# RMS scaling of x one pass earlier, block sums ahead of their splits, a buffer of its own for the seventh block, and earlier evictions in the mixing layer's projections

## The chip, the core and the metric

One core of a Trainium2 chip runs the whole layer as one program. TensorE (PE) multiplies, ScalarE (ACT) and VectorE (DVE) prepare operands and take results out of PSUM, the queue of SyncE (SP) starts the loads from HBM. The metric is the time of the program on the device in microseconds, as the median of several runs. The profiled execution is one more run, with a trace of its own.

## What is computed

A decoder layer of width 2048 over 256 tokens, in float32: a SwiGLU feed-forward of hidden width 5632 at half weight, a mixing layer with one input projection for two groups of heads (RWKV-7 and a gated linear recurrence) and one output projection, a second SwiGLU, and a last RMS norm.

```python
def rms_norm(x, g):
    return x * lax.rsqrt(jnp.mean(x * x, axis=-1, keepdims=True) + NORM_EPS) * g

def swiglu(x, w_gate, w_up, w_down):
    return (jax.nn.silu(x @ w_gate) * (x @ w_up)) @ w_down

h = x
h = h + 0.5 * swiglu(rms_norm(h, ffn1_norm), ffn1_w_gate, ffn1_w_up, ffn1_w_down)
p = rms_norm(h, mix_norm) @ w_in
y_rwkv = rwkv7_time_mix(p[..., :RWKV_IN], ...)
y_lru = rglru_mix(p[..., RWKV_IN:], ...)
h = h + jnp.concatenate([y_rwkv, y_lru], axis=-1) @ w_out
h = h + 0.5 * swiglu(rms_norm(h, ffn2_norm), ffn2_w_gate, ffn2_w_up, ffn2_w_down)
return rms_norm(h, final_norm)
```

## The kernel before

**Products.** Every large product is made of three: an operand is split into a hi part (a cast to fp32r, called whi, xahi, hThi) and a lo part (the operand less its hi part: wlo, xalo, hTlo), and hi x hi, hi x lo and lo x hi are added in a PSUM bank (`three`, L136 to L138; `rows_times`, L174 to L177; `columns_times`, L186 to L188). For a weight, ACT casts (L81, L99) and DVE subtracts (L82, L100). One matmul has 512 columns, or 256 in the mixing layer's projections.

**The feed-forward.** `ffn` runs over the hidden width in chunks: a first one of 512, then five of 1024. In the first chunk the gate product runs over all 16 k tiles (`rows_times`, two k tiles to a split of 1024 columns), then the up product. A further chunk has a gate pass and an up pass of eight pairs of k tiles each, in the order n S n S n S n n. An n step is the plain product of a pair: its halves X1 and X2 are split one after the other, 12 matmuls each. An S step is a product of 2x2 blocks with seven products in place of eight, 21 matmuls. It needs sums of blocks of x (xsums) and of weight blocks (t1 to t4, made by DVE at L125, L127, L128). Its splits are A (b11 and b21), b22 alone (512 columns), C (t1 and t3) and D (t2 and t4); TensorE uses them in this order. After the last S step, DVE and ACT move the shared products into sg or hid (L300 to L304), and at a pass's end the pass's own banks are added (L317, L324). The hidden chunk is transposed by TensorE (L263) and split into hThi and hTlo (L270, L271) in the next chunk's gate pass. Then comes the down product, all with `rows_times`.

**Scaling.** x times its gain is transposed and split before its sum of squares is known. The first chunk's gate pass uses it unscaled, and its Silu (L340) scales by rstd. When the sums of squares are there (L233, `rstd_of`), `spread_rstd` makes rdiag on DVE (L203), a matmul with ones spreads rstd over the partitions (L204) and DVE copies it as rb (L206). In the first chunk's up pass `normalised` takes the pairs of k tiles one by one: DVE adds hi and lo (L279) and multiplies by rb (L280), ACT casts the new hi (L281), DVE subtracts the new lo (L282). For the three pairs of S steps, DVE and ACT go on with the block sums (L286 to L292). The up pass itself still reads unscaled x; its eviction (L351) multiplies by rstd.

**Order and buffers.** A scheduler puts each engine's instructions in order by priority; weight loads, splits and sums have an offset of 4000 over the rest. The order is fixed before the run, and each engine works its list in order. The tiles wst (loads of two k tiles, and t1 to t4), whi and wlo each come from a ring of three buffers (`wpool`). A load waits until the tile three back in its ring has been read.

**The mixing layer.** A projection of four tiles of 128 columns each runs over all k tiles; then DVE multiplies its banks by rb: L571 (raw; for k, r, v of a half of the heads), and in `lru_gate` L935. Between the splits, DVE also does the recurrences: a reciprocal of 128x1024 (L921, twice), a scan (L928) and the inverses of the RWKV part (L754, L758).

## Time and profile before

| | us |
|---|---|
| median of 3 runs | 1953.26 |
| their range | 1949.84 to 1953.41 |
| the profiled execution | 1948.99 |
| its span, first to last instruction | 1947.3 |
| TensorE busy in the span | 1907.3 (98%) |
| VectorE busy | 1440.3 (74%) |
| ScalarE busy | 985.8 (51%) |

By stage, in us of the span: ffn1's first chunk to 62, its passes with S steps from 62 to 503, its down product to 755, the mixing layer's projections and recurrences to about 1140, its output projection and ffn2's first chunk to about 1260, ffn2's S steps to 1700, its down product and the last norm to the end.

How to read it: a matmul's duration in the trace is longer than the distance to the next one, since they are pipelined, so TensorE's busy share does not tell how much of its time is lost. The number of matmuls that start in a stretch does.

### The profile page before, as it was taken

The page shows a single profiled execution, that of the slowest core. Times are in us where ns is not written, and L with a number is a line of the kernel's source. Part 1 is how long each engine was busy: PE and PEld are TensorE (multiplying, and loading weights), DVE is VectorE, ACT ScalarE, POOL GpSimd, SP SyncE. Part 2 cuts the span into 40 slices and gives each one's busy share as a digit, 9 for nine tenths or more (in the row PEclk, how much of TensorE's full clock was granted, in tenths as well). Part 3 has the DMA queues.
Part 4 walks back from the last instruction along what each step waited for, and adds up shares of the span by engine and source line. Part 5 has one row for each costly group of instructions (what it writes and reads, how often), then busy time and mean ns, then how long its engine had stood idle before and what let it go on. Part 6 is the DMA issues. An engine that isn't in the chain of part 4 may idle for free.

```text
span 1947.3 us, 25669 instructions
## 1 busy us (share of the span) xinstructions
PE 1907.3 (98%) x10233; PEld 1589.7 (82%) x10233; DVE 1440.3 (74%) x1822; ACT 985.8 (51%) x1189; POOL 9.9 (1%) x53
## 2 busy tenths in 40 slices
PE   8899999999999999999999999999999999999997
PEld 6678877878888889998899878778888888788886
DVE  5989898888645446876696775899898989844553
ACT  6465555555444335544454555565556555543443
POOL 0000000000000001000000000000000000000000
PEclk9999999999999999999999999999999999999999
DMA  6356555565755556545243456555555655766553
GB/s 238 129 198 214 173 194 195 178 212 190 264 186 204 194 195 207 177 127 163 77 144 115 131 195 215 173 194 182 199 197 198 211 183 184 257 211 193 195 194 129
DMA packets 130032, 360.77 MB, mean 185 GB/s; under 512 B 20879, under 2 KB 23128, under 8 KB 129784
## 3 DMA queue, kind: packets, MB, share of 16 engines
q1 hardware_dynamic: 129592, 358.08, 55.6%
q8 instruction: 80, 1.31, 0.3%
q10 hardware_dynamic: 320, 1.06, 0.1%
q14 instruction: 40, 0.33, 0.0%
HBM read 351.25 MB, written 7.86 MB: 184 GB/s over the span
## 4 chain that ended last, share of the span: by engine, by line
PE 89%; DVE 5%; ACT 3%; issue 2%; DMA 1%; SPq 0%; ACTq 0%; DVEq 0%
PE bank L137 14%; PE bank L136 13%; PE bank L138 13%; PE bank L175 10%; PE bank L177 10%; PE bank L174 10%; PE bank L186 4%; PE bank L188 4%; PE bank L187 4%; ACT whi L99 1%; DVE wlo L82 1%; PE bank L263 1%; DVE wlo L100 1%; PE bank L712 1%; PE bank L640 1%
## 5 line engine op out<-in xcount | busy, mean ns | idle before, releaser
L82 DVE TENSOR_TENSOR wlo<-wst,whi 128x1024 fp32r<-128x1024 f32 (+2 forms) x329 | 398.2, 1212 | 344.6 <-ACT whi L81 343.9
L99 ACT CAST whi<-wst 128x1024 fp32r<-128x1024 f32 (+1 forms) x440 | 430.4, 993 | 364.0 <-PE bank L138 321.9
L81 ACT CAST whi<-wst 128x1024 fp32r<-128x1024 f32 (+2 forms) x329 | 343.2, 1044 | 472.5 <-PE bank L177 335.8
L100 DVE TENSOR_TENSOR wlo<-wst,whi 128x1024 fp32r<-128x1024 f32 (+1 forms) x440 | 493.3, 1147 | 90.9 <-ACT whi L99 85.0
L174 PE MATMUL bank<-whi,hThi 128*128 128x512 f32 x704 | 274.2, 389 | 0.0
L175 PE MATMUL bank<-wlo,hThi 128*128 128x512 f32 x704 | 274.0, 389 | 0.0
L177 PE MATMUL bank<-whi,hTlo 128*128 128x512 f32 x704 | 231.4, 389 | 0.0
L186 PE MATMUL bank<-xahi,whi 128*128 128x256 f32 x688 | 199.1, 290 | 3.2 <-DVE raw L571 3.2
L188 PE MATMUL bank<-xahi,wlo 128*128 128x256 f32 x688 | 197.9, 288 | 0.0
L136 PE MATMUL bank<-whi,xahi 128*128 128x512 f32 x490 | 191.4, 393 | 6.3 <-ACT xahi L281 4.6
L187 PE MATMUL bank<-xalo,whi 128*128 128x256 f32 x688 | 197.3, 287 | 0.0
L137 PE MATMUL bank<-wlo,xahi 128*128 128x512 f32 x490 | 191.5, 391 | 0.6 <-DVE wlo L100 0.6
L136 PE MATMUL bank<-whi,xbhi 128*128 128x512 f32 x490 | 190.2, 391 | 1.9 <-DVE hid L351 1.4
L137 PE MATMUL bank<-wlo,xbhi 128*128 128x512 f32 x490 | 191.1, 390 | 0.6 <-DVE wlo L100 0.6
L138 PE MATMUL bank<-whi,xalo 128*128 128x512 f32 x490 | 191.4, 391 | 0.0
L138 PE MATMUL bank<-whi,xblo 128*128 128x512 f32 x490 | 190.7, 389 | 0.0
L175 PEld LDWEIGHTS bank<-wlo,hThi 128*128 128x128 f32 x704 | 132.2, 188 | 27.4
L177 PEld LDWEIGHTS bank<-whi,hTlo 128*128 128x128 f32 x704 | 132.1, 188 | 27.4
L174 PEld LDWEIGHTS bank<-whi,hThi 128*128 128x128 f32 x704 | 132.2, 188 | 27.1
L186 PEld LDWEIGHTS bank<-xahi,whi 128*128 128x128 f32 x688 | 133.1, 193 | 7.3 <-DVE raw L571 3.6
L188 PEld LDWEIGHTS bank<-xahi,wlo 128*128 128x128 f32 x688 | 132.9, 193 | 1.9 <-issue 1.1
L187 PEld LDWEIGHTS bank<-xalo,whi 128*128 128x128 f32 x688 | 133.1, 194 | 1.2 <-issue 0.2
(298 smaller groups left out, 2557.3 us busy)
## 6 DMA issues: line engine op xcount, KB each, us to landing
wst<-in_ffn_w_up_dram SPq DMA_DIRECT2D x88, 1024.0 KB, 5.0
wst<-in_ffn_w_down_dram SPq DMA_DIRECT2D x88, 1024.0 KB, 4.9
wst<-in_ffn_w_gate_dram SPq DMA_DIRECT2D x87, 1024.0 KB, 5.0
wst<-in_w_in_dram SPq DMA_DIRECT2D x40, 1024.0 KB, 5.0
wst<-in_w_out_dram SPq DMA_DIRECT2D x16, 1024.0 KB, 5.7
h<-parked SPq DMA_DIRECT2D x4, 1024.0 KB, 9.2
wst<-in_w_in_dram SPq DMA_DIRECT2D x4, 640.0 KB, 4.4
h<-in_x_dram SPq DMA_DIRECT2D x4, 512.0 KB, 4.7
```

The lines of the kernel that those rows point to most:

```text
L82: nc.vector.tensor_tensor(lo[:, : m * width], src, hi[:, : m * width].bitcast(F32), ALU.subtract)
L99: self.nc.scalar.copy(hv, src)
L100: self.nc.vector.tensor_tensor(lv, src, hv.bitcast(F32), ALU.subtract)
L136: nc.tensor.matmul(out, a[0], b[0], start=first, stop=False)
L137: nc.tensor.matmul(out, a[0], b[1], start=False, stop=False)
L138: self.last_mm = nc.tensor.matmul(out, a[1], b[0], start=False, stop=last)
L174: nc.tensor.matmul(banks[t][n][:, :w], a, whi[:, c : c + w], start=first, stop=False)
L175: nc.tensor.matmul(banks[t][n][:, :w], a, wlo[:, c : c + w], start=False, stop=False)
L177: self.last_mm = nc.tensor.matmul(banks[t][n][:, :w], b, whi[:, c : c + w], start=False, stop=last)
L186: nc.tensor.matmul(out, a, xhi[:, k, :], start=first, stop=False, skip_group_check=True)
L187: nc.tensor.matmul(out, a, xlo[:, k, :], start=False, stop=False, skip_group_check=True)
L188: nc.tensor.matmul(out, b, xhi[:, k, :], start=False, stop=last, skip_group_check=True)
```

## The change

- *Scaling.* The sums of squares, rstd and `normalised` move into the first chunk's gate pass, from k tile 6 on in ffn1 and from tile 0 on in ffn2. The block sums stay in the up pass (`block_sums`), from scaled pairs that are kept for them in four half tiles of sg and hid (`room`). The up pass now reads scaled x, so the eviction into hid no longer multiplies by rstd. The two loads of further norm gains in ffn1 move with the sums of squares.
- *S steps.* The three sums for t1 to t4 stand in the code before all four splits. b22 has a whi and a wlo tile of its own (tags whb and wlb, one buffer each), so an S step takes three tiles of each ring in place of four.
- *Mixing layer.* The evictions of projections (raw, xb, gate) get a priority offset of 3900. Each reciprocal of 128x1024 becomes four of 128x256.
- *Storage.* xa and xb are held as two halves with tiles of their own; the scrap tile of the sums of squares is float32 and shares its storage with hid. A path for S steps in the down product is there, but its plan is None for all pieces.

```diff
     def split(self, src, n):
-        hi = self.wpool.tile([P, self.WMAX], F32R, name=self.name("whi"), tag="whi")
-        lo = self.wpool.tile([P, self.WMAX], F32R, name=self.name("wlo"), tag="wlo")
+        pool = self.wpool if n == 2 else self.bpool
+        hi = pool.tile([P, n * 512], F32R, name=self.name("whi"), tag="whi" if n == 2 else "whb")
+        lo = pool.tile([P, n * 512], F32R, name=self.name("wlo"), tag="wlo" if n == 2 else "wlb")
...
                 else:
-                    b11, b21 = self.split(b[:, :, 0, :], 2)
-                    (b22,) = self.split(b[:, 1, 1:2, :], 1)
                     tt = self.wpool.tile([P, 2 * self.WMAX], F32, name=self.name("wst"), tag="wst")
                     t = tt.rearrange("p (n f) -> p n f", f=512)
                     nc.vector.tensor_tensor(t[:, 0:2], b[:, :, 1, :], b[:, 0], ALU.subtract)
-                    t1, t3 = self.split(t[:, 0:2], 2)
                     nc.vector.tensor_tensor(t[:, 2], t[:, 1], b[:, 0, 0, :], ALU.add)
                     nc.vector.tensor_tensor(t[:, 3], b[:, 1, 0, :], t[:, 2], ALU.subtract)
+                    b11, b21 = self.split(b[:, :, 0, :], 2)
+                    (b22,) = self.split(b[:, 1, 1:2, :], 1)
+                    t1, t3 = self.split(t[:, 0:2], 2)
                     t2, t4 = self.split(t[:, 2:4], 2)
...
+        norm_at, scaled = 6 if head else 0, 0
         for i, (k, hi, lo) in enumerate(core.weights([(wg, c0, w)], ks, head=bool(head))):
             core.rows_times(gb, xhi, xlo, k, hi, lo, w, i == 0, i == NK - 1)
             if head and i in head:
                 with core.tc.high_priority(offset=3000), core.tc.issue_after(core.last_mm.ins):
                     head[i]()
-        after_first()
-        sg = fpool.tile([P, NT, 1024], F32, name=core.name("sg"), tag="sg")
+            if i == norm_at:
+                after_first()
+                scrap = fpool.tile([P, NT, 1024], F32, name=core.name("sg"), tag="sg")
+                hid = fpool.tile([P, NT, 1024], F32, name=core.name("hid"), tag="hid")
+                sums = rest()
+            if i % 2 and i >= norm_at:
+                while scaled <= i // 2:
+                    normalised(scaled)
+                    scaled += 1
+        sg = scrap
...
-            if i == 0:
-                sums, scrap = rest(), sg
-            if i % 2:
-                normalised(i // 2)
-        hid = fpool.tile([P, NT, 1024], F32, name=core.name("hid"), tag="hid")
+            if i % 2 and i // 2 in place:
+                block_sums(room(i // 2), *sums(place[i // 2]))
         for t in range(NT):
             for n, c, ww in cuts:
-                nc.vector.scalar_tensor_tensor(
-                    hid[:, t, c : c + ww], ub[t][n][:, :ww], rstd[:, t : t + 1], sg[:, t, c : c + ww],
-                    ALU.mult, ALU.mult,
-                )
+                nc.vector.tensor_tensor(hid[:, t, c : c + ww], ub[t][n][:, :ww], sg[:, t, c : c + ww], ALU.mult)
...
-            nc.vector.tensor_tensor(
-                raw[:, :n, 1:257], bk[:, : n * 256].rearrange("p (a s) -> p a s", a=n), self.core.rb[:, None, :].to_broadcast([P, n, 256]), ALU.mult
-            )
+            with self.tc.high_priority(offset=3900):
+                nc.vector.tensor_tensor(
+                    raw[:, :n, 1:257], bk[:, : n * 256].rearrange("p (a s) -> p a s", a=n),
+                    self.core.rb[:, None, :].to_broadcast([P, n, 256]), ALU.mult,
+                )
...
-        nc.vector.reciprocal(D, D)
+        for j in range(4):
+            nc.vector.reciprocal(D[:, j * 256 : (j + 1) * 256], D[:, j * 256 : (j + 1) * 256])
```

The scheduler then puts the instructions in another order. The lists below are parts of it; the first number is the instruction's place on its engine, L the line in the kernel that the list is of, and the numbers behind names tell tiles apart.

TensorE about the start of ffn1's up pass, before: bank_140 is the last bank of the gate pass, bank_369 the first of the up pass, L204 spreads rstd.

```order
104 L175 MATMUL bank_140<-wlo_312,xahi 128x512
105 L177 MATMUL bank_140<-whi_311,xalo 128x512
106 L174 MATMUL bank_369<-whi_373,xahi 128x512
107 L175 MATMUL bank_369<-wlo_374,xahi 128x512
108 L177 MATMUL bank_369<-whi_373,xalo 128x512
109 L174 MATMUL bank_370<-whi_373,xahi 128x512
110 L204 MATMUL bank_349<-rdiag_348,ones 128x128 x2
111 L175 MATMUL bank_370<-wlo_374,xahi 128x512
```

The same place after: whi_326 is the gate pass's last split, whi_364 the up pass's first; L217 spreads rstd, L1137 transposes a norm gain.

```order
76 L217 MATMUL bank_278<-rdiag_277,ones 128x128 x2
77 L187 MATMUL bank_140<-whi_326,xahi_101 128x512
78 L188 MATMUL bank_140<-wlo_327,xahi_101 128x512
79 L190 MATMUL bank_140<-whi_326,xalo_103 128x512
80 L187 MATMUL bank_141<-whi_326,xahi_101 128x512
81 L188 MATMUL bank_141<-wlo_327,xahi_101 128x512
82 L190 MATMUL bank_141<-whi_326,xalo_103 128x512
83 L1137 MATMUL bank_287<-ident,graw_285 128x16
84 L187 MATMUL bank_140<-whi_364,xahi_101 128x512
```

The spreading matmul moved from behind four matmuls of the up pass to six matmuls ahead of it.

DVE about the start of ffn2's up pass, before: wlo_10540 and wlo_10544 are the gate pass's last splits, wlo_10596 and wlo_10600 the up pass's first, L206 makes rb.

```order
1180 L203 TENSOR_SCALAR rdiag_10580<-ident,rstd_96 128x128 x2
1181 L82 TENSOR_TENSOR wlo_10510<-wst_10503,whi_10509 128x1024
1182 L82 TENSOR_TENSOR wlo_10540<-wst_10537,whi_10539 128x1024
1183 L82 TENSOR_TENSOR wlo_10544<-wst_10537,whi_10543 128x1024
1184 L82 TENSOR_TENSOR wlo_10596<-wst_10593,whi_10595 128x1024
1185 L82 TENSOR_TENSOR wlo_10600<-wst_10593,whi_10599 128x1024
1186 L206 COPY rb_10586<-bank_10581 128x256
1187 L280 TENSOR_TENSOR sg_10588<-sg_10588,rb_10586 128x512
```

The same place after: wlo_10567 is the gate pass's last split, wlo_10605 and wlo_10609 the up pass's first; L312 adds hi and lo of a pair of x, L219 makes rb, L313 multiplies by it.

```order
1189 L97 TENSOR_TENSOR wlo_10567<-wst_10560,whi_10566 128x1024
1190 L238 SCALAR_TENSOR_TENSOR xblo_9810<-bank_10435,gT,xbhi_9808 128x256
1191 L255 TENSOR_SCALAR rt_10476<-rt_10476 128x2
1192 L312 TENSOR_TENSOR hid_10490<-xbhi_9808,xblo_9810 128x512
1193 L97 TENSOR_TENSOR wlo_10605<-wst_10602,whi_10604 128x1024
1194 L257 RECIPROCAL rstd_95<-rt_10476 128x2
1195 L216 TENSOR_SCALAR rdiag_10481<-ident,rstd_95 128x128 x2
1196 L219 COPY rb_10487<-bank_10482 128x256
1197 L97 TENSOR_TENSOR wlo_10609<-wst_10602,whi_10608 128x1024
1198 L313 TENSOR_TENSOR hid_10490<-hid_10490,rb_10487 128x512
1199 L313 TENSOR_TENSOR sg_10489<-sg_10489,rb_10487 128x512 x2
```

rb stands behind one split of the up pass where it stood behind two, and adds of pairs of x (there is one more above) stand ahead of it.

DVE in the S steps of ffn1's first full up pass, before: wlo_1062 and wlo_1066 are X1 and X2, wlo_1096 A, wlo_1100 b22, wlo_1106 C and wlo_1112 D of one n step and one S step; wst_1103 holds t1 to t4.

```order
142 L100 TENSOR_TENSOR wlo_1062<-wst_1059,whi_1061 128x1024
143 L100 TENSOR_TENSOR wlo_1066<-wst_1059,whi_1065 128x1024
144 L125 TENSOR_TENSOR wst_1103<-wst_1093 128x1024
145 L100 TENSOR_TENSOR wlo_1096<-wst_1093,whi_1095 128x1024
146 L127 TENSOR_TENSOR wst_1103<-wst_1103,wst_1093 128x512
147 L100 TENSOR_TENSOR wlo_1100<-wst_1093,whi_1099 128x512
148 L128 TENSOR_TENSOR wst_1103<-wst_1093,wst_1103 128x512
149 L100 TENSOR_TENSOR wlo_1106<-wst_1103,whi_1105 128x1024
150 L100 TENSOR_TENSOR wlo_1112<-wst_1103,whi_1111 128x1024
```

The same two steps after: wlo_1065 and wlo_1069 are X1 and X2, wlo_1103 A, wlo_1107 b22, wlo_1111 C, wlo_1115 D.

```order
142 L116 TENSOR_TENSOR wlo_1065<-wst_1062,whi_1064 128x1024
143 L136 TENSOR_TENSOR wst_1098<-wst_1096 128x1024
144 L116 TENSOR_TENSOR wlo_1069<-wst_1062,whi_1068 128x1024
145 L137 TENSOR_TENSOR wst_1098<-wst_1098,wst_1096 128x512
146 L116 TENSOR_TENSOR wlo_1103<-wst_1096,whi_1102 128x1024
147 L138 TENSOR_TENSOR wst_1098<-wst_1096,wst_1098 128x512
148 L116 TENSOR_TENSOR wlo_1107<-wst_1096,whi_1106 128x512
149 L116 TENSOR_TENSOR wlo_1111<-wst_1098,whi_1110 128x1024
150 L116 TENSOR_TENSOR wlo_1115<-wst_1098,whi_1114 128x1024
```

The first sum (L136) went ahead of X2 and the third (L138) ahead of b22. On ACT b22's cast (whi_1106) now stands ahead of A's, here after X1 and X2:

```order
94 L115 CAST whi_1064<-wst_1062 128x1024
95 L115 CAST whi_1068<-wst_1062 128x1024
96 L115 CAST whi_1106<-wst_1096 128x512
97 L115 CAST whi_1102<-wst_1096 128x1024
98 L115 CAST whi_1110<-wst_1098 128x1024
99 L115 CAST whi_1114<-wst_1098 128x1024
```

Before, A's cast (whi_1095) stood ahead of b22's.

## Rows read from the trace of the kernel before

**Rows 1.** The page's busy line: us (share of span) xinstructions.

```profile
PE 1907.3 (98%) x10233; PEld 1589.7 (82%) x10233; DVE 1440.3 (74%) x1822; ACT 985.8 (51%) x1189; POOL 9.9 (1%) x53
```

**Rows 2.** TensorE's waits: line, releaser, total us, times, longest.

```profile
PE bank L136 <- ACT xahi L281: 4.6, 1, 4.6
...
PE bank L186 <- DVE raw L571: 3.2, 2, 3.0
...
PE bank L175 <- DVE wlo L82: 2.2, 3, 1.1
```

**Rows 3.** TensorE by stretch: length, busy (matmuls), granted clock, DMA share, GB/s.

```profile
60.00:80.00 20.00, 12.97 (x47) 0.83 0.32 105
880.00:900.00 20.00, 16.95 (x117) 0.91 0.69 197
1260.00:1280.00 20.00, 18.67 (x76) 1.00 0.45 154
100.00:500.00 400.00, 399.07 (x1763) 1.00 0.60 198
1300.00:1700.00 400.00, 399.48 (x1764) 1.00 0.59 198
1760.00:1920.00 160.00, 160.00 (x708) 1.00 0.58 192
```

**Rows 4.** The same, transposes of L263 alone.

```profile
100.00:500.00 400.00, 9.05 (x72) 1.00 0.60 198
1300.00:1700.00 400.00, 8.27 (x69) 1.00 0.59 198
```

**Rows 5.** One S step in order of time: start, duration, engine, line, [idle before].

```profile
487.25 0.39 PE L136 MATMUL bank<-whi,xahi 128*128 128x512 f32 x1
...
489.29 0.61 PE L136 MATMUL bank<-whi,xsums 128*128 128x512 f32 x2
489.86 0.50 PE L137 MATMUL bank<-wlo,xsums 128*128 128x512 f32 x1
490.19 0.40 PE L138 MATMUL bank<-whi,xsums 128*128 128x512 f32 x1
...
487.49 1.05 ACT L99 CAST whi<-wst 128x1024 fp32r<-128x1024 f32 x1 [2.14 <-PE bank L138]
...
488.57 3.72 DVE L100 TENSOR_TENSOR wlo<-wst,whi 128x1024 fp32r<-128x1024 f32 x3 [1.55 <-ACT whi L99]
```

**Rows 6.** DVE by line and shape, 100 to 500 us: busy us, mean ns.

```profile
L100 DVE TENSOR_TENSOR wlo<-wst,whi 128x1024 fp32r<-128x1024 f32 x176 | 209.9, 1220 | 43.9 <-ACT whi L99 41.8
...
L128 DVE TENSOR_TENSOR wst<-wst,wst 128x512 f32<-128x512 f32 x27 | 18.5, 686 | 0.3
```

**Rows 7.** Loads of weights in the passes with S steps.

```profile
DMA to landing us min/median/max: 4.8/5.0/5.8
```

**Rows 8.** ffn1's first chunk on TensorE, in order of time.

```profile
38.97 0.68 PE L204 MATMUL bank<-rdiag,ones 128*128 128x128 f32 x4 [0.62 <-DVE rdiag L203]
...
63.04 0.47 PE L136 MATMUL bank<-whi,xahi 128*128 128x512 f32 x1 [1.69 <-DVE hid L351]
...
69.38 0.80 PE L136 MATMUL bank<-whi,xahi 128*128 128x512 f32 x1 [4.56 <-ACT xahi L281]
```

**Rows 9.** DVE by stretch: length, busy (instructions), granted clock, DMA share, GB/s.

```profile
20.00:40.00 20.00, 11.41 (x14) 1.00 0.52 163
100.00:500.00 400.00, 353.67 (x395) 1.00 0.60 198
1220.00:1240.00 20.00, 12.48 (x21) 1.00 0.63 198
```

**Rows 10.** ffn2's first chunk in order of time, DVE and then TensorE.

```profile
1236.87 0.42 DVE L206 COPY rb<-bank 128x256 f32<-128x256 f32 x1 [0.86 <-PE bank L204]
...
1260.02 0.47 PE L136 MATMUL bank<-whi,xbhi 128*128 128x512 f32 x1 [1.38 <-DVE hid L351]
...
1262.33 0.50 PE L136 MATMUL bank<-whi,xbhi 128*128 128x512 f32 x1 [0.51 <-ACT xbhi L281]
```

More of the change, by code (lines that the diff above doesn't have):

```diff
@@ L19, with __init__, __getitem__ @@
 EPS = 1e-6
+class Halves:
+    def __init__(self, *tiles):
+        self.tiles = list(tiles)
+    def __getitem__(self, at):
+        rows, k, cols = at
+        if isinstance(k, slice):
+            i, k = k.start // 8, slice(k.start % 8, k.start % 8 + k.stop - k.start)
+        else:
+            i, k = k // 8, k % 8
+        return self.tiles[i][rows, k, cols]
 class Core:
@@ L101, in split, with pairs @@
         return [(hi[:, i * 512 : i * 512 + 512], lo[:, i * 512 : i * 512 + 512]) for i in range(n)]
-    def pairs(self, mat, c0, plan):
+    def pairs(self, mat, c0, plan, ids):
         nc = self.nc
-        ns = plan.count("S")
-        ids = {"S": iter(range(ns)), "n": iter(range(ns, self.NK // 2))}
-        for kind in plan:
-            p = next(ids[kind])
+        for kind, p in zip(plan, ids):
             with self.tc.high_priority(offset=4000):
@@ L157, in rows_times_pairs @@
                 self.three(aux[0], x(0, 0), w["b11"], f, l)
-                self.three(own[1], sm(3), w["b22"], first, last)
-                self.three(aux[1], sm(0), w["t1"], f, l)
-                self.three(aux[3], sm(2), w["t3"], f, l)
-                self.three(aux[2], sm(1), w["t2"], f, l)
+                self.three(own[1], sm(4), w["b22"], first, last)
+                self.three(aux[1], sm(1), w["t1"], f, l)
+                self.three(aux[3], sm(3), w["t3"], f, l)
+                self.three(aux[2], sm(2), w["t2"], f, l)
                 self.three(own[2], x(1, 1), w["t4"], first, last)
@@ L243, in rstd_of, with ffn @@
         nc.vector.reciprocal(rstd, tmp)
-def ffn(core, xhi, xlo, rstd, wg, wu, wd, after_first, after_down, fpool, down, rest, back, head=None):
+def ffn(core, xhi, xlo, rstd, wg, wu, wd, after_first, after_down, fpool, down, rest, back, spare, head=None):
     nc, NT, NK, D, S = core.nc, core.NT, core.NK, core.D, core.S
@@ L1045 @@
 HIDDEN_AT = 6
+DOWN_PLAN, DOWN_HIDDEN_AT = (None, None, None), 2
 @with_exitstack
@@ L1084, in xt_pool, with half, sums @@
         pool = stack.enter_context(tc.tile_pool(name=name, bufs=1, **kw))
-        return [pool.tile([P, NK, S], F32R, name=name + n) for n in ("hi", "lo")]
+        def half(n, i):
+            return pool.tile([P, NK // 2, S], F32R, name=core.name(name + n), tag=f"{n}{i}")
+        def sums():
+            tiles = [pool.tile([P, 4, 512], F32R, name=core.name(name + "sum"), tag=f"{n}1") for n in ("hi", "lo")]
+            return lambda p: tuple(t[:, p % 4, :] for t in tiles)
+        return [Halves(half(n, 0), half(n, 1)) for n in ("hi", "lo")], half, sums
     with ExitStack() as front:
-        xa = xt_pool(front, "xa")
+        xa, xa_half, xa_sums = xt_pool(front, "xa")
         with ExitStack() as st:
```

139 lines of the change are left out of this document (91 added, 48 removed).

## The prediction, made before the changed kernel ran

> **What bounds the kernel now.** I read the page's busy line first: TensorE is busy for 98% of the span, VectorE (DVE) for 74%, ScalarE (ACT) for 51% [rows 1]. So the end is set by TensorE, and since the change leaves its matmuls as they are (8947 rows before, 8948 after, in the lists of instructions), all it can bring is TensorE time that is now lost. The list of what TensorE waited for says where the long waits are [rows 2]: one of 4.6 us for x scaled (L281), 3.2 us for a projection's eviction (L571), 2.2 us for weight splits, and others at the first hidden chunks. The list leaves out short waits, so I then counted matmuls by stretch [rows 3]. In a part of the down projection with nothing but matmuls of 512 columns, 708 start in 160 us, 0.226 us each. In the 400 us of passes with S steps in ffn1, 1763 start, of which 72 are transposes that take 9.05 us [rows 4]: 1691 x 0.226 + 9.05 = 391.2, so 8.8 us are lost. The same sum for ffn2 (1764, 69 transposes) gives 1695 x 0.226 + 8.27 = 391.3, 8.7 us lost. The two stretches with S steps are some 425 us long each, so about **19 us** go there, in pieces too short for the list.
>
> One S step shows the piece [rows 5]. The two L136 that open t1 and t3 start at 489.29 and 0.226 later, the next matmul (wlo of t1) should come at 489.74. It starts at 489.86, and the one after that 0.33 later instead of 0.23: 0.22 us lost. What it waited for is the subtraction that starts on DVE at 488.57 (1.22 us), behind the cast on ACT at 487.49, which had stood idle for 2.14 us for "PE bank L138": the whi buffer of C (t1, t3) is the one that the n step's second half (X2) holds until TensorE starts the S step. An S step takes four buffers (A: b11, b21; b22; C; D: t2, t4) of a ring of three. There are 60 S steps (3 in each of 20 passes): at 0.22 to 0.31 (the first of a pass loses a little more) 13 to 19 us, most or all of it.
>
> **The change part by part.**
>
> *Ring of three for three (S steps).* b22 gets its own buffer, so C takes the buffer of X1, free 12 matmuls (2.7 us) sooner, and D that of X2. Per pair n + S, TensorE needs 45 x 0.226 = 10.2 us. From the moment the matmul behind a buffer's last one starts (487.25 for X2) it is 0.24 to the cast's start, then 1.05 cast and 1.22 subtraction [rows 5], 2.5 us in all. D: X2 free at 0 (S step's start), ready at 2.5, wanted at 16 matmuls = 3.6. The next X1, in A's buffer: free at 1.4 (6 matmuls), ready 3.9, wanted 5.0. The next X2, in C's: free at 3.4, ready 5.9, wanted 7.7. So no buffer is late by itself: the margin is 1.1 us or more. What is late next is DVE: five splits and, as long as a split, the sum of 1024 columns, 6 x 1.22, and 3 x 0.69 for the others make 9.4 us of 10.2 per pair [rows 6], and in it the loop of the load. The pair's wst buffer is free when b22's subtraction ends; the load takes 5.0 us at the median, 5.8 at most [rows 7], so some 5.15 with its two signals; then, by the new order, come sum (1.14 start to start), X2's subtraction (1.14), sum (0.61), A (1.14), sum (0.61), b22 (0.61): 10.4 us against 10.2, where the old order (sum, A, sum, b22, sum behind X2) makes 9.3. A pass has three S steps and then two n steps that need no sums, and 3 x 0.2 stays under the margin of 1.1; but loads scatter, so I charge half the overshoot, 0.1, to each of 60 steps, 6 us, and 3 us for what stays at the passes' ends, where evictions and transposes wait for each other. Of 19 us **10 come back**; bounds 4 (the loop costs its 0.2 in full on each step, and the ends the same) and 15 (margins hold, only the ends stay).
>
> *x scaled in ffn1's first gate pass.* The count of matmuls in 60 to 80 us is 47, where 88 fit: 9.3 us lost [rows 3]. The waits there are 1.69 at 63.04 and 4.56 at 69.38 [rows 8]; of the rest, some 0.6 is a third wait and some 2.5 us TensorE at 1.2 GHz (granted clock 0.83 in that stretch) and restarts. Another microsecond goes at 38.97 [rows 8]. DVE had idled for 8.6 of the 20 us before 40 [rows 9], and only then got rb. By the order, the matmul that spreads rstd moves from the 4th matmul of the up pass to 6 before it, 10 x 0.226 = 2.3 us, and its own wait of 0.62 goes, since the split ahead of it on DVE ends 2.9 us before the up pass (its buffer is left 24 matmuls, 5.4 us, before the pass, and 2.5 us go from there to the subtraction's end). Two of the adds (0.69 each) are done before rstd is there. DVE is thus some 2.9 + 1.4 = 4.3 us ahead, and the waits of 6.8 us shrink by that; of the lost clock I give back 0.7. **5 us**, bounds 2 (the wait for pair 1's lo part, now behind more splits, takes over) and 8. The first gate pass still reads x unscaled, and its Silu still scales, so no instruction is added.
>
> First the row, for the clock: after the idle of 4.56 us and after that of 3.0 in front of L571 the granted clock of the stretch is 0.83 and 0.91; after 1.38 at 1260.02 it stays at 1.00 [rows 2, 3, 8, 10]. The Trainium skill (TensorE: Matmul & The Clock Gate, "HAM oscillation — how this bites in real kernels") says that idle gaps between bursts send the array back to half rate; by it a long wait that is left in ffn1 would keep the whole 2.5 us of clock loss, and this term would be 4.3.
>
> *The same in ffn2.* DVE idles 7.5 us of the 20 before 1240 [rows 9], and rb came at 1236.87 [rows 10]. By the order it stands behind the first split of the up pass instead of the second, and the spreading matmul 11 matmuls (2.5 us) ahead of the pass; there it waits some 0.3 us for that split. DVE is some 2.1 + 1.4 us ahead of before, and the waits at 1260.02 and 1262.33 [rows 10] with a smaller one between, 2.5 us, go, less the new 0.3: **2 us**, bounds 0 and 4.
>
> *Mix.* The evictions get a priority just under that of the splits. In the order the eviction behind the 3.2 us wait (k, second half) stands where it stood, between the same two splits: nothing there. The gate's evictions move ahead of the scan, and a reciprocal of 8x256 behind a split that waited 1.1 us [rows 2]; 0.4 of it goes and that wait also loses its restart. Each of the two long reciprocals becomes four with splits between; no long TensorE wait stands behind one now. Price of six more instructions: 2 x 0.69 - 1.22 = 0.16 each [rows 6], 1.0 us of DVE at most, nothing where DVE idles. Net **+0.5**, bounds -3 (one more wait like L571's, elsewhere) and +3.
>
> The Trainium skill (Perfetto Trace Analysis, "Optimizing Scalar/DVE Operations") puts an access overhead of some 60 ns on a DVE instruction and advises larger ones where the engine is saturated. By that estimate the six cost 0.4 us; the rows' 0.16 is more, and the measurement decides.
>
> *The rest.* Silu's partner at L351 loses a scalar operand; junk becomes f32 in another pool; the down path is the old one (its plan is None). No price: same instructions, same queues, ACT 51% busy.
>
> **Sum.** 10 + 5 + 2 + 0.5 = 17.5 us. Against the profiled execution (1948.99) 1931.5; the median of the runs lies 4.3 us above it, which would make 1935.8. I take **1933**.
>
> **The rivals.**
>
> *DVE and the load loop bind the S passes.* For: 9.4 of 10.2, a loop of 10.4. Against: DVE idles 46 us of 400 there [rows 9], and two n steps per pass let it catch up. Then S steps give 0 to 4 and the rest 7: 1940 to 1946, say 1943.
>
> *The scaling only moves its wait.* The sums stay in the up pass, and xalo of pair 1 is still behind weight splits. Then 10 + 0.5: 1942.
>
> *Slower: the sum ahead of the splits on an in-order DVE.* The first sum of an S step now stands ahead of X2's (in each pass's first S step of X1's) subtraction. If the load comes late, DVE waits for it with those subtractions queued behind, which TensorE wants first. With a load of 5.0 us it costs the 0.1 above. With 5.8, the longest of before, for all, the loop is 11.2, 1.0 over: 3 x 1.0 - 1.1 = 1.9 us on each of 20 passes, and the 3 at the ends, 41 us lost against 19 now, less 7.5 won elsewhere: 1953 + 22 - 7.5 = 1968. It decides where 3 times the overshoot less 1.1 is over 1.2, from a load of 5.6 us. Against it: the median is 5.0.
>
> *Everything fits*: 15 + 8 + 4 + 3 = 30: 1920.
>
> **How the numbers follow.** Forecast (1924 to 1940) 0.54; DVE binds 0.20; scaling moves its wait 0.12; all fits 0.07; slower 0.07. The range 1920 to 1948 takes in the upper end of the second case (4 + 2 + 0 - 3 = 3 us under the profiled run, rounded up toward the median); outside it are the slow case, and what no row shows. 0.2% is 3.9 us, about what a measurement can tell. Faster 0.85: all but the slow case and a piece of the second (0.08, no difference); slower 0.07.
>
> **What would show it.** In 100 to 500 us the matmuls should rise from 1763 to about 1784, without the pattern of 0.33 behind L137 of t1; if DVE's sum waits for a load there, the slow rival is at work. In 60 to 80 the count should rise from 47 to about 68; a wait of some 2 us for xalo would be the one that is left. At 1260 no wait over 0.5. The wait at L571 (3 us) should be there as before; were it gone, the order didn't tell what I read from it. Wrong would be the whole if the S stretches' count stays.

## The result and the profile after

The changed kernel takes **1931.38 us** (median of 4 runs, 1929.94 to 1935.32) where the kernel before takes 1952.19 (median of 4 beside it, 1949.84 to 1953.41): a ratio of 0.9898, 95% interval 0.988 to 0.9916. The profiled execution is the run of 1929.94, the shortest of the four, with a span of 1928.2.

The page's busy line, which answers to [rows 1]: TensorE is busy 12.2 us less, DVE and ACT within 2 us of before.

```profile
PE 1895.1 (98%) x10233; PEld 1598.7 (83%) x10233; DVE 1440.9 (75%) x1828; ACT 984.0 (51%) x1189; POOL 9.7 (1%) x53
```

TensorE's waits (line, releaser, total us, times, longest), which answer to [rows 2]:

```profile
PE bank L199 <- DVE raw L633: 3.6, 2, 3.1
...
PE bank L190 <- DVE xalo L315: 2.2, 1, 2.2
...
PE bank L217 <- DVE xalo L238: 1.5, 1, 1.5
...
PE bank L946 <- DVE rs L930: 1.0, 1, 1.0
```

The wait of 4.6 us for xahi is gone, and one of 2.2 for xalo is there in its place; the wait for the projection's eviction (L571 before, now L633) is what it was; L946 is new. L217, which spreads rstd, also waited before (L204):

```profile
PE bank L204 <- DVE xalo L225: 0.9, 1, 0.9
```

TensorE by stretch (length, busy and matmuls, granted clock, DMA share, GB/s), which answers to [rows 3]:

```profile
40.00:60.00 20.00, 17.85 (x72) 0.91 0.43 149
60.00:80.00 20.00, 20.00 (x89) 1.00 0.48 157
866.00:886.00 20.00, 16.95 (x110) 0.83 0.70 197
1260.00:1280.00 20.00, 20.00 (x89) 1.00 0.77 250
100.00:500.00 400.00, 399.53 (x1791) 1.00 0.59 204
1280.00:1680.00 400.00, 398.39 (x1782) 1.00 0.59 202
```

The same for the transposes of L280 alone (L263 before), which answers to [rows 4]:

```profile
100.00:500.00 400.00, 9.42 (x72) 1.00 0.59 204
1280.00:1680.00 400.00, 8.98 (x72) 1.00 0.59 202
```

The prediction's count of lost time, on these: in ffn1's S passes (1791 - 72) x 0.226 + 9.42 = 397.9, so 2.1 us of 400 are lost where 8.8 were; in ffn2's (1782 - 72) x 0.226 + 8.98 = 395.4, 4.6 lost where 8.7 were. The busy column (399.07 before, 399.53 after) shows nothing of that; the count of matmuls does.

Two S steps of the changed kernel, which answer to [rows 5] (start, duration, engine, line), at products with xsums:

```profile
157.83 0.50 PE L149 MATMUL bank<-whi,xsums 128*128 128x512 f32 x1
158.17 0.40 PE L150 MATMUL bank<-wlo,xsums 128*128 128x512 f32 x1
...
166.39 0.39 PE L149 MATMUL bank<-whi,xsums 128*128 128x512 f32 x1
166.62 0.39 PE L150 MATMUL bank<-wlo,xsums 128*128 128x512 f32 x1
166.84 0.39 PE L151 MATMUL bank<-whi,xsums 128*128 128x512 f32 x1
167.07 0.39 PE L149 MATMUL bank<-whi,xsums 128*128 128x512 f32 x1
```

From 166.39 on the starts are 0.23 apart through all four products, where before one was 0.33. At 157.83, in the last of the four, a piece of 0.11 is left (0.34 instead of 0.23).

By stages, from the starts of the same matmuls in each trace (us; "head" is up to the 66th matmul of the first chunk with S steps, in ffn2 counted from the start of the mixing layer's output projection; e2 to e11 are the experiments below):

| | before | after | e2 | e3 | e5 | e9 | e11 |
|---|---|---|---|---|---|---|---|
| ffn1 head | 85.8 | 79.0 | 80.2 | 79.0 | 75.3 | 89.3 | 77.4 |
| ffn1 S passes | 417.2 | 410.4 | 416.6 | 411.7 | 421.0 | 410.7 | 418.4 |
| ffn1 down | 243.1 | 243.0 | 243.0 | 243.0 | 243.0 | 243.0 | 243.0 |
| mixing, to its output projection's start | 368.3 | 371.3 | 370.2 | 370.1 | 369.5 | 375.2 | 374.6 |
| output projection and ffn2 head | 163.5 | 159.0 | 159.9 | 160.5 | 158.9 | 164.4 | 159.7 |
| ffn2 S passes | 416.7 | 412.4 | 416.4 | 412.7 | 418.5 | 413.0 | 420.1 |

What lies behind them is equal within 0.2 us. After against before: -6.8, -6.8, 0, +3.0, -4.4, -4.2, in all 19.2 us, the difference of the spans (1947.3 - 1928.2 = 19.1). Of the 4.4 us, 0.7 are the output projection's (98.1 us before, 97.5 after) and 3.7 those of ffn2's first chunk (65.2 and 61.5). e5's heads are short because its long wait comes behind the 66th matmul, in the S passes; there the two rows go together.

### The profile page after: what moved, and what is told of

It is laid out like the page before. It is cut to its first block, busy times and chain, and to the rows that moved or that the text cites. A ratio compares the mean times of both kernels' runs of the same rounds, so it can differ in the third digit from the quotient of the medians.

```text
span 1928.2 us, 25657 instructions
## 1 busy us (share of the span) xinstructions
PE 1895.1 (98%) x10233; PEld 1598.7 (83%) x10233; DVE 1440.9 (75%) x1828; ACT 984.0 (51%) x1189; POOL 9.7 (1%) x53
## 4 chain that ended last, share of the span: by engine, by line
PE 86%; DVE 8%; DMA 3%; issue 2%; ACT 1%; SPq 0%; DVEq 0%; ACTq 0%
PE bank L149 12%; PE bank L151 12%; PE bank L150 12%; PE bank L190 11%; PE bank L188 11%; PE bank L187 11%; PE bank L199 4%; PE bank L200 4%; PE bank L201 4%; DVE wlo L116 2%; DMA wst<-in_ffn_w_gate_dram 2%; DVE wlo L97 1%; PE bank L280 1%; PE bank L775 1%; DVE hid L365 1%
## 5 line engine op out<-in xcount | busy, mean ns | idle before, releaser
L116 DVE TENSOR_TENSOR wlo<-wst,whi 128x1024 fp32r<-128x1024 f32 (+1 forms) x440 | 499.5, 1147 | 58.1 <-ACT whi L115 52.2
```

Source lines behind the costliest of these rows:

```text
L116: self.nc.vector.tensor_tensor(lv, src, hv.bitcast(F32), ALU.subtract)
```

## The experiments

Times are medians; the kernel before ran on the same chip beside each of them. Changes are against the changed kernel where nothing else is said. The changed kernel itself was not run again beside them. By the ratios to the kernel before, what comes out as 10.5 (e1), 10.5 (e2), 9.3 (e5 against e3), 18.2 (e9) and 13.9 us (e11) by the medians is 8.6, 9.4, 9.0, 16.4 and 13.5.

**e1: S steps as before.** b22's own buffer and the place of the sums are undone.

```diff
-        pool = self.wpool if n == 2 else self.bpool
...
+        hi = self.wpool.tile([P, self.WMAX], F32R, name=self.name("whi"), tag="whi")
+        lo = self.wpool.tile([P, self.WMAX], F32R, name=self.name("wlo"), tag="wlo")
...
+                    b11, b21 = self.split(b[:, :, 0, :], 2)
+                    (b22,) = self.split(b[:, 1, 1:2, :], 1)
                     tt = self.wpool.tile([P, 2 * self.WMAX], F32, name=self.name("wst"), tag="wst")
...
+                    t1, t3 = self.split(t[:, 0:2], 2)
```

> The changed kernel with its S-step part undone: b22 back in the ring of three, the sums t1 to t4 back between the splits; scaling and mixing layer as changed. Theory (the stall of C behind X2's buffer is worth some 11 us in all, as the two traces say): 1942 us, and the matmuls that start in 100 to 500 us fall from 1791 to about 1765. Rival (the S steps' stall went because the pass starts with DVE ahead after the earlier scaling): 1932 to 1935, the count stays near 1790.

Measured: 1941.84 us (1937.36 to 1942.9), ratio to before 0.9942 (0.9929 to 0.9954). The S steps' part is worth 10.5 us.

**e2: the buffer alone undone.** The first hunk of e1, without the second.

```diff
-        pool = self.wpool if n == 2 else self.bpool
...
+        hi = self.wpool.tile([P, self.WMAX], F32R, name=self.name("whi"), tag="whi")
+        lo = self.wpool.tile([P, self.WMAX], F32R, name=self.name("wlo"), tag="wlo")
```

> The changed kernel with only b22's own buffer undone (four tiles of the ring per S step again); the sums stay ahead of the splits in the code. Theory (the buffer is what counts): like the kernel with the whole S part undone, some 1941 us, with the 0.33 us step behind t1's lo matmul back. Rival (the sums made ahead of the splits are what counts): 1931 to 1934.

Measured: 1941.91 us (1939.39 to 1942.62), 0.9946 (0.9934 to 0.9959). Without the buffer the early sums bring nothing: the count in the two long stretches goes back to that of [rows 3].

```profile
100.00:500.00 400.00, 399.60 (x1766) 1.00 0.59 198
...
1280.00:1680.00 400.00, 399.60 (x1765) 1.00 0.59 197
```

**e8: the buffer kept, the sums back between the splits.** The other half of e1.

```diff
+                    b11, b21 = self.split(b[:, :, 0, :], 2)
+                    (b22,) = self.split(b[:, 1, 1:2, :], 1)
                     tt = self.wpool.tile([P, 2 * self.WMAX], F32, name=self.name("wst"), tag="wst")
...
+                    t1, t3 = self.split(t[:, 0:2], 2)
```

> The changed kernel with b22's own buffer kept and the sums t1 to t4 back between the splits. Theory (the buffer is all of the S part's gain): 1931 to 1934 us. Rival (with the sums late, C's and D's casts wait for DVE in place of the buffer): 1937 to 1942 us.

Measured: 1929.78 us (1927.47 to 1931.3), 0.9888 (0.9876 to 0.99). So the whole gain of the S steps is the buffer's. That e8 is 1.6 us ahead isn't shown to be the sums': its S passes are no shorter (410.1 and 413.5 us, against 410.4 and 412.4). Its head of ffn1 is 1.4 us shorter (77.6), and there the wait for xalo is the same, but TensorE did not drop to 1.2 GHz behind it in this execution. e8's wait (line, releaser, total us, times, longest), then its stretch, to be held against 72 matmuls at 0.91 above:

```profile
PE bank L190 <- DVE xalo L315: 2.2, 1, 2.2
```

```profile
40.00:60.00 20.00, 17.85 (x79) 1.00 0.43 145
```

7 matmuls x 0.226 = 1.6 us.

**e11 and e12: a load that lands later.** The 1 MB of an S step's pair is loaded in four pieces of 256 KB, in the changed kernel (e11) and in the kernel before (e12).

```diff
-                nc.sync.dma_start(
-                    out=st.rearrange("p (k f) -> p k f", k=2),
...
+                for q in range(4 if kind == "S" else 1):
+                    w4 = 1 if kind == "S" else 4
+                    kq, nq = (slice(q // 2, q // 2 + 1), slice(q % 2 * 512, q % 2 * 512 + 512)) if w4 == 1 else (slice(0, 2), slice(0, 1024))
+                    nc.sync.dma_start(
+                        out=st.rearrange("p (k f) -> p k f", k=2)[:, kq, nq],
```

> The changed kernel with the load of an S step's pair (1 MB) issued as four loads of 256 KB one behind the other, so that the whole lands about 1 us later. It tests the loop of the load in the prediction (load, sum, X2, sum, A, sum, b22 on DVE against 10.2 us of TensorE for a pair of steps). By that loop a load of 6 us and more costs 3 x 1.0 less 1.1 on each of 20 passes, some 38 us and the ends: 1955 to 1985. Rival (the queue of loads runs far enough ahead that the sum's wait on DVE is hidden by the order of splits): within 4 us of the changed kernel, 1930 to 1935.

> The kernel before the change with the same four loads for an S step's pair. By the loop of the prediction the old order has 9.3 us against 10.2, so 1 us later costs at most 0.1 on a step, 0 to 6 us: 1950 to 1958. Rival (the order of the sums makes no difference to what a late load costs): the same loss as with the changed kernel.

Measured: e11 1945.24 us (1943.23 to 1948.96), 0.9967 (0.9956 to 0.9977); e12 1953.86 (1949.54 to 1955.73), 1.0003 (0.9994 to 1.0012). The changed kernel loses 13.9 us, the old one 1.3 beside a median of 1952.54. In the S passes e11 loses 8.0 + 7.7 us, e12 nothing (416.5 and 416.9 us for the two stages). So the changed kernel has the loop that the prediction wrote down, and the kernel before does not show it. That this is the order's doing is not shown: e12 also has the ring without b22's own buffer, its S passes take 6.1 and 4.4 us longer than the changed kernel's as e2's do, and so a late load has more room there. The old order with b22's own buffer (e8) was not run with the load in four. Its trace with the whole load points to the order: 15 of its 60 sums wait for a load, 9.3 us in all, where 34 wait 21.9 us in the changed kernel. DVE in the changed kernel, then in e11, at the same two steps (start, duration, [idle before]):

```profile
158.83 1.22 DVE L136 TENSOR_TENSOR wst<-wst 128x1024 f32<-128x1024 f32 x1
...
169.39 1.23 DVE L136 TENSOR_TENSOR wst<-wst 128x1024 f32<-128x1024 f32 x1 [0.44 <-DMA wst<-in_ffn_w_gate_dram]
```

```profile
159.59 1.22 DVE L139 TENSOR_TENSOR wst<-wst 128x1024 f32<-128x1024 f32 x1
...
170.61 1.22 DVE L139 TENSOR_TENSOR wst<-wst 128x1024 f32<-128x1024 f32 x1 [0.94 <-DMA wst<-in_ffn_w_gate_dram]
```

From sum to sum it is 10.56 us in the changed kernel and 11.02 in e11, against 10.2 of TensorE. The load in four came only some 0.5 us later there, not 1, and neither range of e11's expectation was met. With 0.4 over on an S step little reaches TensorE (2.1 and 4.6 us were lost in the two stretches), by the prediction's reading because the n steps at the pass's end catch up; with 0.8 over, 15.7 us in 20 passes do, 0.8 on each, where 3 x 0.8 - 1.1 = 1.3 was the prediction's form. The Trainium skill (Perfetto Trace Analysis, "DMA Optimizations") says that splitting a DMA into smaller pieces may let some of them start sooner, and the whole finish sooner where the DMA engines are generally idle. That condition does not hold here, since the DMA share of these stretches is 0.59 (rows above). The first sum needs the whole pair, and by the sums' starts the four pieces came later as a whole. TensorE's waits in e11 name the places, splits, transposes and hTlo at the passes' ends among them (lines are three higher there):

```profile
PE bank L153 <- DVE wlo L116: 6.9, 10, 1.4
...
PE bank L283 <- DVE sg L335: 2.9, 4, 0.8
...
PE bank L152 <- DVE hTlo L291: 2.1, 3, 1.1
```

**e3: x scaled in the up pass again,** with its four half tiles and the block sums behind each pair's matmuls kept.

```diff
-            if i == norm_at:
-                after_first()
...
-                sums = rest()
-            if i % 2 and i >= norm_at:
-                while scaled <= i // 2:
-                    normalised(scaled)
...
+            if i == 0:
+                sums = rest()
+            if i % 2:
+                normalised(i // 2)
```

> The changed kernel with the scaling of x back in the up pass of the first chunk (both feed-forwards), all else as changed. Theory (ffn1's first chunk gave 8 us, ffn2's 3): 1941 to 1943 us, with waits of 4 to 5 us at the first S steps of ffn1. Rival (the wait only moved, as its rest of 2.15 us for xalo and the half clock behind it hint): 1934 us or less.

Measured: 1932.62 us (1931.7 to 1935.7), 0.9906 (0.9891 to 0.9921). The earlier place is worth 1.2 us, less than the intervals tell apart. My theory had 10 there and fell: what the diff shows first, the move into the gate pass, is not what the time came from.

**e5: e3 with one scratch tile** for all pairs, and so the block sums at once behind each pair's scaling, as in the kernel before.

```diff
+        if p in place:
+            hi, lo = sums(place[p])
...
-        at = place.get(p, 3)
-        return (scrap, hid)[at // 2][:, at % 2, 512:].rearrange("p (k s) -> p k s", k=2)
+        return scrap[:, 0, 512:].rearrange("p (k s) -> p k s", k=2)
```

> The kernel of the run before last (scaling back in the up pass, the rest as changed), and the scaled pairs again in one scratch tile with the block sums in a second one, as before the change, in place of four half tiles. Theory (new, from that run: where the scaling is done hardly counts; the one scratch tile made each pair wait for the last reader of the pair before it, DVE waiting on ACT's cast, and the four half tiles took that away): 1938 to 1940 us, with the waits of 4 to 5 us for L314's cast back at the second S step of ffn1. Rival (the S steps' own buffer and the sums made first took ffn1's waits away): 1932 to 1934 us.

Measured: 1941.91 us (1940.15 to 1944.38), 0.9952 (0.994 to 0.9965), 9.3 us above e3. The long wait for xahi of [rows 2] and the stretch with half of its matmuls missing [rows 3] are back, 20 us later:

```profile
PE bank L149 <- ACT xahi L314: 5.5, 1, 5.5
```

```profile
80.00:100.00 20.00, 14.48 (x51) 0.83 0.31 106
```

With one tile the add of the next pair (DVE) waits until the last pair's cast (ACT), its subtraction and its block sums have read the tile. DVE's busy time in 34 to 54 us, in e3 and then in e5, shows what that costs it:

```profile
34.00:54.00 20.00, 17.25 (x31) 1.00 0.55 187
```

```profile
34.00:54.00 20.00, 13.64 (x24) 1.00 0.54 180
```

These 3.6 us of DVE's work are missing later. From 72 us until the add behind the long wait starts (86.08), DVE works on splits and sums with hardly a gap.

**e6: the kernel before with three tiles in turn,** and nothing else: block sums stay where they were.

```diff
-        tmp = scrap[:, 0, 512:].rearrange("p (k s) -> p k s", k=2)
+        tmp = (scrap[:, 0], hid[:, 0], hid[:, 1])[p % 3][:, 512:].rearrange("p (k s) -> p k s", k=2)
```

> The kernel before, with one edit: the scratch of a scaled pair goes round three half tiles (one of sg, two of hid) in place of one. Theory (the tiles alone bring ffn1's first chunk forward): 1944 to 1947 us, the stretch from 60 to 80 us up from 47 matmuls to over 70. Rival (they bring nothing without the earlier scaling or the S part): 1951 to 1953 us.

Measured: 1948.88 us (1946.6 to 1951.73, 12 runs) beside 1951.2 of before (16 runs), 0.9988 (0.9979 to 0.9996). Only 2.3 us: the count in 60 to 80 rises from 47 to 61, but the waits go over to weight splits (L136 <- ACT whi L99: 4.7 us, 5 times) and ffn2's head loses. So tiles alone don't do it. What e3 has over e6 is the fourth tile and the block sums put off until behind a pair's matmuls, which one tile doesn't allow; which of these two carries the rest was not taken apart.

**e9: the changed kernel with one scratch tile,** x still scaled in the gate pass. The diff is that of e5, on the changed kernel instead of e3.

> The changed kernel with x still scaled in the gate pass, but with one scratch tile for all pairs in place of four half tiles, so the block sums are made at once behind each pair's scaling, as before the change. Theory (the four half tiles are what counts, since with one tile the add of the next pair on DVE waits for the work of ACT on the last pair): a wait of 3 us or more for xahi or xalo stays at the head of the up pass or moves into the gate pass, and the time is 1937 to 1941. Rival (either of the two is enough: with the earlier start the chain of one tile is hidden behind the gate pass): no such wait, 1930 to 1933.

Measured: 1949.6 us (1947.42 to 1950.34), 0.9982 (0.9973 to 0.999). It is dearer than I expected: 18.2 us above the changed kernel, and nearly all of the change's gain. Its up pass runs at the pace of the chain over one tile, with the weight splits between its links; three waits, 9.0 and 9.5 us apart and two pairs each, and the stretch's clock:

```profile
40.53 0.51 PE L187 MATMUL bank<-whi,xahi 128*128 128x512 f32 x1 [1.65 <-ACT xahi L314]
...
49.57 0.50 PE L187 MATMUL bank<-whi,xahi 128*128 128x512 f32 x1 [1.70 <-ACT xahi L314]
...
59.04 0.50 PE L187 MATMUL bank<-whi,xahi 128*128 128x512 f32 x1 [1.70 <-ACT xahi L314]
```

```profile
40.00:60.00 20.00, 15.92 (x52) 0.83 0.39 127
```

Of the 20.4 us between the two spans, 10.3 are ffn1's head and 5.4 ffn2's. The 3.9 in the mixing layer go with a drop of TensorE's clock. From the 64 small products of inv and gram to the first product of uv and gram behind them, the changed kernel takes 10.8 us (1031.79 to 1042.59) and e9 15.2 (1041.83 to 1056.99), with the same matmuls in the same order. TensorE waits for nothing there; its granted clock falls. The same happened in e7, e10 and e11. The stretch in the changed kernel, e9, e7 and e10:

```profile
1030.00:1050.00 20.00, 19.38 (x307) 1.00 0.34 107
```

```profile
1040.00:1060.00 20.00, 20.00 (x229) 0.74 0.32 107
```

```profile
1020.00:1040.00 20.00, 20.00 (x219) 0.75 0.32 106
```

```profile
1030.00:1050.00 20.00, 19.69 (x275) 0.83 0.17 57
```

The four kernels together, where e9's time holds some 4 us of that drop in its profiled execution:

| | one scratch tile, sums at once | four half tiles, sums later |
|---|---|---|
| scaled in the up pass | 1941.91 (e5) | 1932.62 (e3) |
| scaled in the gate pass | 1949.6 (e9) | 1931.38 (after) |

**e7: the scaling ahead of the weight splits** in priority, to take away the 2.2 us wait that is left.

```diff
-                    normalised(scaled)
+                    with core.tc.high_priority(offset=4300):
+                        normalised(scaled)
```

> The changed kernel with the scaling in the gate pass at a priority just over that of weight splits (4300 against 4000), so that the lo parts of pairs 1 to 3 stand ahead of two splits they stood behind. Theory (the wait of 2.15 us for xalo in ffn1's up pass and the half clock behind it, 3.9 us in all, is what the early scaling loses again): 1927.5 to 1929 us, no wait over 0.5 us there. Rival (the splits behind them are then late by as much): 1931 to 1933 us.

Measured: 1930.57 us (1928.21 to 1932.1), 0.9892 (0.9878 to 0.9905). The wait is gone and ffn1's head is 2.2 us shorter, but ffn2's is 0.3 longer and the mixing layer 2.4; in all no difference that can be told. The mixing layer's 2.4 are less than what the drop of the clock shown under e9 took of this execution, 4.3 us.

**e4: the mixing layer's part undone:** no priority for evictions, whole reciprocals.

```diff
-            with self.tc.high_priority(offset=3900):
...
-        for j in range(4):
-            nc.vector.reciprocal(D[:, j * 256 : (j + 1) * 256], D[:, j * 256 : (j + 1) * 256])
+        nc.vector.reciprocal(D, D)
```

> The changed kernel with the mixing layer as before: evictions without priority, each long reciprocal whole. Theory (this part brought nothing: the projections' stage is 3 us longer in the trace, half of it a longer half-clock stretch behind the same wait of 3.1 us, 1.1 us a new wait before L946): 1929 to 1931 us. Rival (the forecast's +0.5 us gain, the longer stage being the clock's alone): 1932 us.

Measured: 1930.35 us (1930.05 to 1931.24), 0.989 (0.9876 to 0.9903): this part brings nothing that can be told. By stage it gives 0.7 us in the output projection (98.2 in e4, 97.5 after) and costs 0.8 ahead of it (370.6 and 371.4).

**e10: a candidate,** e8's order of sums, e7's priority in ffn1 only, and one copy on ACT instead of DVE, ahead of the eviction that TensorE waits 3.1 us for.

```diff
-        nc.vector.tensor_copy(XT, X.rearrange("q s t -> q t s"))
+        nc.scalar.copy(XT, X.rearrange("q s t -> q t s"))
```

> A candidate for a faster kernel: the changed one with the sums back between the splits (the first sum still first), x scaled ahead of the splits in ffn1 only, and the copy of invw (L825, 64x1024, 1.03 us on DVE) on ACT, so that the eviction of k's second half in front of which TensorE waits 3.1 us stands one instruction earlier. Theory: the gains add up, 1.6 from the sums, 2.2 from ffn1's first pass and 1 to 2 from the eviction: 1926 to 1928. Rival: the wait for k's eviction only changes its releaser, and the half clock behind it stays: 1928.5 to 1930.5.

Measured: 1927.96 us (1925.25 to 1929.34), 0.9871 (0.9858 to 0.9885). It is the shortest of all, 3.4 us under the changed kernel by the medians; the two intervals still overlap by 0.0005, and it is not told apart from e8 (1929.78). The copy takes 2.00 us on ACT where it took 1.03 on DVE, and the wait falls from 3.06 to 1.97, with the clock at full rate behind it (first DVE in the changed kernel, then in e10 ACT, TensorE and TensorE's stretch, to be held against 110 matmuls at 0.83 in the changed kernel):

```profile
871.18 1.03 DVE L825 COPY invw<-inv 64x1024 f32<-64x1024 f32 x1
```

```profile
871.51 2.00 ACT L826 COPY invw<-inv 64x1024 f32<-64x1024 f32 x1 [2.85 <-DVE inv L822]
```

```profile
873.25 0.39 PE L199 MATMUL bank<-xahi,whi 128*128 128x256 f32 x1 [1.97 <-DVE raw L634]
```

```profile
866.00:886.00 20.00, 17.30 (x132) 1.00 0.67 197
```

Behind this eviction e10 is 1.8 us ahead of e8, which has the copy on DVE. Nothing of that is left at the stage's end, since the clock's drop in the recurrences (shown under e9) takes it back: up to its output projection the mixing layer takes 369.6 us in e10 and in e8, 1.8 less than in the changed kernel. In ffn1's head a wait of 1.0 us for a split took the place of the one for xalo, and the head is as long as in the changed kernel (79.3 against 79.0).

## Why the prediction was right, step by step

**The sum.** 17.5 us were forecast against the profiled execution, and 19.2 came. Its terms came out as 11.0 for 10 (S passes), 6.8 for 5 (ffn1's head), 3.7 for 2 (ffn2's first chunk) and -2.3 for +0.5 (mixing layer with its output projection). That the sum lies so near is in part luck: three terms were too low by 1.0, 1.8 and 1.7 us, and the fourth too high by 2.8.

**S steps: right in size and mechanism.** The reading of [rows 5], four buffers of a ring of three, is what e2 shows: the buffer alone is worth 10.5 us. The pattern of 0.33 behind L137 is gone but for a rest of 0.11, and 1791 matmuls for the forecast 1784 start in 100 to 500. The charge of 9 us for what stays was near too: 2.1 + 4.6 us per 400. Its reason was only half right. The sum that now stands ahead of X2's split does wait for its load, and little of that reaches TensorE. DVE's waits over the whole program (line, releaser, total us, times, longest):

```profile
DVE wst L136 <- DMA wst<-in_ffn_w_gate_dram: 11.5, 17, 2.0
DVE wst L136 <- DMA wst<-in_ffn_w_up_dram: 10.4, 17, 1.2
```

34 of 60 sums wait, 0.6 us each. The loop of 10.4 us was worked out well: 10.56 from one sum to the next, which waits. Of that, 5.26 lie between the end of b22's subtraction (164.13) and the sum's start, where the prediction put 5.15 for the load with its signals, without a row for the signals. DVE's 9.4 of 10.2 us are too much, since they add up durations, which overlap; by the distances from start to start that the prediction uses for the loop (1.14 and 0.61) they are 8.7. e11 shows that the rival of the late load is a real edge: half a microsecond more, and 13.9 us go. It was priced too high by some 1.7 times (1.3 for 0.8 a pass). The early sums thus bring more waits for loads on DVE and, by e2 and e8, no gain.

**ffn1's head: the size held, the cause did not.** The prediction took the scaling's earlier place for the cause: rstd spread sooner, DVE 4.3 us ahead. That came as read: the spreading matmul of 38.97 [rows 8] now has its copy rb done at 31.8. Yet e3, with x scaled in the up pass, is within 1.2 us. The step that failed is the one that was not there: the four half tiles and the later block sums stood in the description of the change and got no price (9.3 us by e5, in both feed-forwards), because the wait of 4.56 us [rows 8] was read as DVE being late by rb alone, when DVE was, by e5, late from taking turns with ACT over one tile, with the block sums in between. Its releaser, ACT's cast of xahi, names the other engine of that chain; I went to DVE's idle time instead. What would be left was named rightly, a wait of some 2 us for xalo behind splits. DVE, then TensorE:

```profile
31.40 0.42 DVE L219 COPY rb<-bank 128x256 f32<-128x256 f32 x1
...
40.99 2.50 DVE L97 TENSOR_TENSOR wlo<-wst,whi 128x1024 fp32r<-128x1024 f32 x2
43.41 0.68 DVE L315 TENSOR_TENSOR xalo<-sg,xahi 128x512 fp32r<-128x512 f32 x1
```

```profile
44.15 1.22 PE L190 MATMUL bank<-whi,xalo 128*128 128x512 f32 x2 [2.15 <-DVE xalo L315]
45.17 0.63 PE L187 MATMUL bank<-whi,xahi 128*128 128x512 f32 x1
```

xalo stands behind two splits (2.50 us). In 40 to 80 us 161 matmuls start where 135 did (88 and 47); in 60 to 80 alone it is 89, where 68 was forecast. By the Trainium skill (TensorE: Matmul & The Clock Gate, "HAM oscillation — how this bites in real kernels") the clock loss would stay and the term be 4.3; a drop did stay in this execution (0.91), and the term came out larger all the same.

**ffn2's head: half the size, and the cause only in part.** The price was the sum of the waits that the trace names, 2.5 us [rows 10]. The count would have given more: 76 matmuls of 88 in 1260 to 1280 [rows 3] are 2.7 us, and 83 in the 20 before another 1.1. Now there are 89 and 88. By this count the waits cost 1.3 us more than their own length. The 20 us before, in the kernel before:

```profile
1240.00:1260.00 20.00, 18.64 (x83) 1.00 0.40 122
```

The earlier place is worth 1.5 us of the 3.7 by e3, whose first chunk takes 63.0 us where the changed kernel's takes 61.5; that is near the forecast 2. What gave the rest was not taken apart: in e5 the one tile costs ffn2's first chunk and S passes together 4.3 us against e3.

**Mixing layer: as read, but the end was near the lower bound.** The wait at L571 stayed (3.05, now 3.06), as the order told, and e4 makes the part nothing, 1.0 the other way. What the term was priced for came, 0.7 us in the output projection. Ahead of it the stage is 3.0 us longer in the profiled execution, and in e4, with the part undone, 2.2 longer, so most of that is not the part's. A new wait of 1.0 (L946 for rs) is in it, which e4 does not have, and so is the clock behind the old wait. The 7 us behind it, before and then after (granted clock third):

```profile
886.60:893.60 7.00, 6.98 (x41) 0.76 0.73 195
```

```profile
874.00:881.00 7.00, 7.00 (x35) 0.56 0.61 182
```

0.2 x 7 is 1.4 us. Another 0.6 is the wait of the matmul that spreads rstd for this layer (L217, 1.5 us; L204 before, 0.9); e4 has it too. Smaller waits that came and went are left out of this. The price of 0.16 us for an added DVE instruction was taken from durations, which overlap; the distances from start to start (0.61 and 1.14) give 0.08, nearer the 0.4 us for all six that the prediction set aside.

**The rivals.** That scaling only moves its wait was right about the move and wrong about the time, since the tiles came with it. DVE and the load loop bind S steps only when the load is later (e11).

## What to carry to other kernels

A ring that lacks one buffer for the steps that share it costs a fraction of a microsecond on each, hardly shows in a list of waits, and is found by counting instructions that start against those that would fit. When a chain crosses two engines through one scratch tile, price the tile, and the work that reads it, before the place where the chain starts: here one pass earlier gave 1 us with more tiles and later sums, and without them 9.3 us were lost in one place and 18.2 in the other. When a stage gets longer that nobody edited, look at its granted clock first: some 4 us of e9 and of e7 were that. An operation that moves ahead of others on an in-order queue should earn something there, because it also brings its own late input to them.

## What the runs showed of the hardware

The length of a wait of about 2 us doesn't tell whether TensorE drops to 1.2 GHz behind it. The same 2.15 us wait for xalo ended in a drop in the changed kernel (0.91, matmuls of 0.63 us) and in none in e8 (1.00). Waits of 1.97 (e10, at 873.25) and, in ffn2's head of e9, of 2.10 had none; one of 1.65 in e9 had one (0.83). The one of 2.10, and its stretch:

```profile
1253.41 0.50 PE L187 MATMUL bank<-whi,xbhi 128*128 128x512 f32 x1 [2.10 <-ACT xbhi L314]
```

```profile
1240.00:1260.00 20.00, 17.44 (x73) 1.00 0.49 159
```

The Trainium skill (TensorE: Matmul & The Clock Gate, "HAM oscillation — how this bites in real kernels") says that waits between bursts of matmuls, when they are long enough, send the array back to half rate. The drops behind the waits of 3 us and more that stand in this text agree with it (0.83 to 0.91); e8, e9 and e10 have waits of about 2 us without one.

A drop needs no wait, either. In the recurrences of the second half of the mixing layer the clock fell in the profiled executions of e7, e9, e10 and e11 (0.74 to 0.83 over 20 us) with no wait in front. What TensorE did before it fell were 64 products of 32x32, 2.2 us in all in the changed kernel. With the same matmuls in the same order as in e7, e9 and e11 it stayed at 1.00 in the changed kernel, e1, e2, e3, e5 and e8. Why it fell in the one and not in the other is open.

What is worth carrying is the size: the drop in ffn1's head cost 1.6 us, behind a wait of 2.15, and the one in the recurrences of e7, e9 and e11 4.3 to 4.4.
